# Modulation vectors of two transformer blocks: from TensorE products and partition sums to VectorE row sums

## The chip, the cores and the metric

One core of one Trainium2 chip. The metric is the device time of one execution in microseconds (us); the three runs of the kernel before gave 2533.99, 2531.1 and 2531.23, their median is 2531.23.

## What is computed

Two blocks, each of two layers, run one after the other on an input of 256 tokens by 1024 channels (f32). Every layer scales, shifts and gates its activations with vectors of 1024 that depend on a condition alone (6 chunks in a layer of the first block, 9 in one of the second):

```python
cond = silu(c)                                   # first block, [1, 1024]
mod = cond @ ada_w[layer] + ada_b[layer]         # [1, 6*1024]: shift, scale, gate (mixer), shift, scale, gate (FFN)
h = rmsnorm(x, norm_mix_g[layer]) * (1 + scale_m) + shift_m
x = x + gate_m * mixer(h)
h = rmsnorm(x, norm_ffn_g[layer]) * (1 + scale_f) + shift_f
x = x + gate_f * swiglu(h, ffn_w_in[layer], ffn_w_out[layer])
# second block: two streams (x with condition c_2, ctx with c_ctx_2), 9 chunks of 1024
m = (silu(cond) @ w_mod + b_mod).reshape(9, 1024)
```

The mixer is attention in layer 0 of the first block, a gated delta rule in layer 1, and a mix of Fourier, convolution and latent attention in the second block, which has an FFN before and one after it. `ada_w` is 2 x 1024 x 6144, `w_mod_2` 2 x 1024 x 9216; both are read from HBM once, as every other weight. The output is the x stream, 256 x 1024.

## The kernel before, in words

Activations lie transposed: eight tiles `x[k]` of 128 channels by 512 columns (256 of x, 256 of ctx). All weights are packed by the host into one array of units in the order in which they are used. `plan()` (L98) writes that order out by hand: a list of units, each a tile of 128 partitions by up to 1024 columns (512 KB). A "mat" unit is for matmuls; a "mod" or "acc" unit holds 128 rows of one chunk of a modulation matrix, so a chunk is eight units. `_evenly` (L57) strews the modulation units among the mat units of a stage, `_spread` (L47) puts one behind each.

`pump` (L373) runs up to 12 units ahead of the place in the plan. It issues the loads on SyncE's queue (L379) into two rings of buffers, 6 for mat units and 3 (`RAWM`) for modulation units, and it splits the next three mat units into a high and a low part, a cast on ScalarE (ACT, L391) and a subtraction on VectorE (DVE, L392); five such pairs of buffers exist. `get` (L397) hands a split unit to the matmuls, and before it `flush` (L405) works off the modulation units that stand ahead of it. A product of f32 quality is three matmuls on TensorE (PE), high x high, high x low and low x high (`mm3`, L414, lines 418 to 420). The tile framework sets the semaphores; each engine's queue runs in order.

A modulation unit is worked off in `mod_unit` (L482) in one of two ways. Kind "mod": four matmuls with 32 columns of the condition as weights, one for each quarter of 256 columns, summed in a PSUM buffer of their own over the eight units (`mod_rows`, L512, line 514). Kind "acc": an accumulator of 128x1024 takes on unit times condition, first by ACT (L501), then by a multiply-add on DVE (L508); in the first block's FFNs ACT multiplies (L505) and GpSimd (POOL) adds (L506). After the eighth unit `settle` (L517) sums over the partitions with four matmuls for each condition (L514 again). In both cases `mod_end` (L527) copies the result out (L531), transposes it with two matmuls (L534) so that the 1024 values lie as 128 partitions by 8 columns, and adds the bias (L542). Kind "mod" are chunks 1, 0, 4, 5 of layer 0 and 2, 3, 4, 5 of layer 1 of the first block; the other 22 chunks are "acc".

Stages in time, with the chunks that are worked off in them: start (1 and 0 of layer 0, before the first matmul unit), attention (2, 3 strewn, 4 and 5 behind the output projection), first FFN (layer 1's 0, 1), delta rule (2, 3, 4 strewn, 5 at its end), second FFN (second block's 1, 0), two-stream FFN (7 chunks), mix, two-stream FFN (5), two-stream FFN (6), mix, last FFN (none). The eight PSUM buffers are 3 "mm", 3 "ax", one "nm" for norms and one "md" for modulations.

At the start DVE computes the tables of the rotary embedding (`rope_tables`, L725, from L731 on) as soon as the positions have landed, then the norm (L568 to L570), the scaling of x (L897); the shift (L904 on ACT, L905 on DVE) needs chunk 0.

Of the kernel before, what the change touches and what calls it, by code (L numbers as in the profile page):

```python
# [34 lines left out]
def _mods(name, l, ch):  # L35
    return [("mod", (name, l, ch, kt), [(name, l, kt * 128, ch * 1024, 1024)]) for kt in range(KT)]
# [10 lines left out]
def _spread(units, mods, every):  # L47

    out, mods = mods[:3], mods[3:]
    for i, u in enumerate(units):  # L50
        out.append(u)
        if i % every == every - 1 and mods:
            out.append(mods.pop(0))
    return out + mods


def _evenly(units, mods, a, b, kind="acc"):  # L57

    n = len(units) - a - b
    out, k = [], 0  # L60
    for i, u in enumerate(units):
        out.append(u)
        while k < len(mods) and i >= a + k * n // len(mods):
            out.append((kind,) + mods[k][1:])
            k += 1
    return out
# [31 lines left out]
def plan():  # L98
# [15 lines left out]
    u += _evenly(q, A(0, 2, 3), 4, 0)  # L114
    q = []
# [4 lines left out]
    u += _spread(q, A(0, 4, 5), 1)  # L120
    u += _evenly(_ffn_units(("f", 0), "ffn_w_in", "ffn_w_out", 0), A(1, 0, 1), MODS_IN, MODS_OUT)
# [6 lines left out]
    u += _evenly(q, A(1, 2, 3, 4), 0, 4, "mod")  # L128
    u += A(1, 5)
# [16 lines left out]
def pack_weights(inp):  # L146
# [5 lines left out]
    arr["gdn_ab"] = ab  # L152
    arr["w_kr"] = np.tile(inp["w_in_2"][:, :, 1664:1696], (1, 1, 4))
# [25 lines left out]
def _col_plan():  # L179
    o = 0  # L180
    for name, n in (("norm_mix_g", 16), ("norm_ffn_g", 16), ("ada_b", 96), ("final_norm_g", 8),
                    ("gdn_conv", 96), ("gdn_norm_g", 1), ("a_log", 1), ("dt", 1), ("c", 8),
                    ("b_mod_2", 144), ("ffn1_norm_2", 16), ("mix_norm_2", 16), ("ffn2_norm_2", 16),
                    ("final_norm_2", 8), ("conv_w_2", 12), ("q_norm_2", 6), ("kv_norm_2", 4),
                    ("c_2", 8), ("c_ctx_2", 8), ("inv_freq", 1)):
        COLS[name] = (o, n)
        o += n
    return o
# [5 lines left out]
def pack_cols(i):  # L194
# [5 lines left out]
    def lay(v):  # L200
# [10 lines left out]
        "a_log": pad(i["gdn_a_log"][0]), "dt": pad(i["gdn_dt_bias"][0]), "c": _vec(i["c"][0]),  # L211
        "b_mod_2": lay(i["b_mod_2"]), "ffn1_norm_2": lay(i["ffn1_norm_2"]), "mix_norm_2": lay(i["mix_norm_2"]),
        "ffn2_norm_2": lay(i["ffn2_norm_2"]), "final_norm_2": _vec(i["final_norm_2"]), "conv_w_2": conv2,
        "q_norm_2": lay(i["q_norm_2"]), "kv_norm_2": lay(i["kv_norm_2"]), "c_2": _vec(i["c_2"][0]),
        "c_ctx_2": _vec(i["c_ctx_2"]), "inv_freq": invc,
# [72 lines left out]
class Unit:  # L288
    def __init__(self, hi, lo):
# [6 lines left out]
             "macc": (1024, 1), "sm": (512, 2), "e": (768, 1), "pt": (768, 1), "tab": (512, 1), "t": (256, 2)},  # L296
    "ffn1": {"hb": (KT * 520, 1), "t": (256, 3), "s": (256, 4), "hid": (512, 11), "macc": (1024, 2), "mprod": (1024, 1)},
# [12 lines left out]
class Builder:  # L310
    RAW, RAWM, SPL = 6, 3, 5
    LOOK, LOOKS = 12, 3

    def __init__(self, tc, es, a):
# [16 lines left out]
        self.unsettled = None  # L331
# [37 lines left out]
    def ax(self):  # L369
        return self.psum("ax", 3)  # L370
# [34 lines left out]
    def flush(self, n=len(PLAN)):  # L405

        end = self.pos + n
        while self.pos < min(end, len(PLAN)) and PLAN[self.pos][0] != "mat":
            self.pump()
            r = self.raw.pop(self.pos)  # L410
            self.mod_unit(PLAN[self.pos][1], r, PLAN[self.pos][0] == "acc")
# [70 lines left out]
    def mod_unit(self, key, r, acc):  # L482


        self.settle()
        name, l, ch, kt = key
        s0, ns = (0, 1) if name == "ada_w" else (1, 2)
        if kt == 0:
            if acc:
                self.macc = [self.t("macc") for _ in range(ns)]  # L490
            else:
                self.pmod = self.psum("md", 1)
        if not acc:
            self.mod_rows(self.pmod, self.cond[:, kt, :], r, kt == 0, kt == KT - 1)
            if kt == KT - 1:
                self.mod_end(key, self.pmod)
            return
        for s, a in enumerate(self.macc):
            w = self.cond[:, kt, s0 + s:s0 + s + 1]
            if kt == 0:  # L500
                self.nc.scalar.activation(a, r, AF.Copy, scale=w)  # L501
                continue
            if ns == 1 and "mprod" in self.tags:
                t = self.t("mprod")
                self.nc.scalar.activation(t, r, AF.Copy, scale=w)  # L505
                self.nc.gpsimd.tensor_tensor(a, a, t, op=OP.add)  # L506
            else:
                self.nc.vector.scalar_tensor_tensor(a, r, w, a, op0=OP.mult, op1=OP.add)  # L508
        if kt == KT - 1:
            self.unsettled = key, s0, self.macc  # L510

    def mod_rows(self, p, w, r, start, stop):  # L512
        for g in range(4):
            self.nc.tensor.matmul(p[32 * g:32 * g + 32, :256], w, r[:, 256 * g:256 * g + 256],  # L514
                                  start=start, stop=stop)

    def settle(self):  # L517

        if self.unsettled is not None:
            key, s0, acc = self.unsettled  # L520
            self.unsettled = None
            p = self.psum("md", 1)
            for s, a in enumerate(acc):
                self.mod_rows(p, self.pick[:, s0 + s, :], a, s == 0, s == len(acc) - 1)
            self.mod_end(key, p)

    def mod_end(self, key, p):  # L527
        nc = self.nc
        name, l, ch, _ = key
        e = self.sm.tile([128, 256], F32, name=f"me{name}{l}{ch}", tag="me", bufs=1)  # L530
        nc.scalar.copy(e, p[:, :256])  # L531
        q = self.psum("md", 1)
        for h in range(2):
            nc.tensor.transpose(q[:, 128 * h:128 * h + 128], e[:, 128 * h:128 * h + 128], self.ident)  # L534
        v = q[:, :256].rearrange("p (h g q) -> p g h q", h=2, g=4)
        ns = 1 if name == "ada_w" else 2
        t = self.keep(8 * ns, f"mod_{name}_{l}_{ch}")
        o, _ = COLS["ada_b" if ns == 1 else "b_mod_2"]
        nch = 6 if ns == 1 else 9
        b = self.cols[:, o + (l * nch + ch) * 8:o + (l * nch + ch) * 8 + 8]  # L540
        for s in range(ns):
            nc.vector.tensor_tensor(t[:, 8 * s:8 * s + 8].rearrange("p (g h) -> p g h", h=2),  # L542
                                    v[:, :, :, s if ns == 1 else 1 + s],
                                    b.rearrange("p (g h) -> p g h", h=2), op=OP.add)
            if ns == 2 and ch in (2, 8):
                nc.vector.tensor_scalar(t[:, 8 * s:8 * s + 8], t[:, 8 * s:8 * s + 8], 0.5, None, op0=OP.mult)
        self.mod[name, l, ch] = t
# [121 lines left out]
    def ffn(self, key, st, ns, A, B, gate, more, before_last=None):  # L669
# [55 lines left out]
    def rope_tables(self):  # L725
        nc = self.nc
        pi = self.sm.tile([128, T], I32, name="pos_i", tag="me", bufs=1)
# [211 lines left out]
    def gdn_gates(self, h):  # L939
        nc = self.nc  # L940
        p = self.gemm(self.get(("ab",)), h, 0, T)
        z, e, g = self.t("ga"), self.t("ga"), self.t("ga")
# [670 lines left out]
```

## Time and profile before

| | |
|---|---|
| median of three runs | 2531.23 us |
| the profiled execution, its own time | 2531.74 us |
| its span, first to last instruction | 2529.8 us |
| instructions | 39830 |
| moved by DMA | 407.59 MB, mean 161 GB/s |

Durations are those of the profiled execution. The profile's engines: PE is the matmul part of TensorE and PEld its weight loads, DVE is VectorE, ACT ScalarE, POOL GpSimd, SP SyncE, which only issues loads here. "L508" is line 508 of the kernel; a "<-" names what a tile is made from, or who ended a wait. A matmul in f32 shows as two records. Matmuls overlap, so the mean duration of one is longer than the time it takes of PE.

### The profile page before, as it was taken

How to read it: one execution, taken by the hardware profiler on the slowest of the kernel's cores; microseconds unless marked ns; L12 is line 12 of the kernel's file. 1: busy time of each engine (PE TensorE's matmuls, PEld its weight loads, DVE VectorE, ACT ScalarE, POOL GpSimd, SP SyncE). 2: the span in 40 equal slices, each digit the busy share in tenths (PEclk: the TensorE clock that was granted, in tenths of full speed). 3: DMA queues.
4: the chain of work that ended last, by engine and by line, in shares of the span. 5: the costliest groups of instructions: out<-in, count | busy, mean ns of one | idle time of the engine just before them, and what ended most of it. 6: DMA issues, size and time to landing. Idle time of an engine off the chain costs nothing.

```text
span 2529.8 us, 39830 instructions
## 1 busy us (share of the span) xinstructions
PE 2472.3 (98%) x15855; PEld 2155.0 (85%) x15855; DVE 1679.2 (66%) x2585; ACT 1127.6 (45%) x1957; POOL 199.8 (8%) x191
## 2 busy tenths in 40 slices
PE   7998999999999999999999999999999999999998
PEld 5878998988999877778886888888888888888998
DVE  6857768765887966775557564565556665576765
ACT  4556556665644532333437432323432323455544
POOL 1004100413100100000010100000100000111000
PEclk9999999999999999999999999999999999999999
DMA  9767656323876455554221243454244453232552
GB/s 339 269 206 250 205 188 226 109 92 122 302 244 207 169 166 174 193 189 151 90 71 42 76 153 108 144 173 147 101 158 156 154 173 125 84 127 84 199 184 93
DMA packets 117113, 407.59 MB, mean 161 GB/s; under 512 B 12992, under 2 KB 16320, under 8 KB 116928
## 3 DMA queue, kind: packets, MB, share of 16 engines
q1 hardware_dynamic: 113904, 402.30, 46.7%
q10 hardware_dynamic: 3024, 2.75, 0.4%
q8 instruction: 125, 2.05, 0.3%
q14 instruction: 60, 0.49, 0.1%
HBM read 403.95 MB, written 1.05 MB: 160 GB/s over the span
## 4 chain that ended last, share of the span: by engine, by line
PE 92%; DVE 3%; ACT 1%; DMA 1%; issue 1%; POOL 1%; DVEq 0%; ACTq 0%; POOLq 0%
PE pmm L418 26%; PE pmm L420 25%; PE pmm L419 25%; PE pmd L514 2%; PE pax L1070 2%; PE pmm L1392 1%; PE pax L420 1%; PE pax L419 1%; PE pax L418 1%; DMA r<-w 1%; PE pnm L1431 1%; PE pax L1402 1%; DVE l L392 1%; PE pnm L605 1%; PE pmm L427 0%
## 5 line engine op out<-in xcount | busy, mean ns | idle before, releaser
L391 ACT CAST h<-r 128x1024 fp32r<-128x1024 f32 (+2 forms) x543 | 548.7, 1016 | 1022.0 <-PE pmm L419 947.3
L392 DVE TENSOR_TENSOR l<-r,h 128x1024 fp32r<-128x1024 f32 (+2 forms) x543 | 656.4, 1214 | 307.8 <-ACT h L391 298.5
L418 PE MATMUL pmm<-h,h 128*128 128x512 f32 (+1 forms) x1916 | 669.8, 351 | 6.7 <-ACT h L638 2.3
L419 PE MATMUL pmm<-h,h 128*128 128x512 f32 (+1 forms) x1916 | 663.9, 347 | 2.0 <-DVE h L639 1.9
L420 PE MATMUL pmm<-h,l 128*128 128x512 f32 (+1 forms) x1916 | 664.5, 347 | 1.0 <-DVE l L392 1.0
L418 PEld LDWEIGHTS pmm<-h,h 128*128 128x128 f32 x1916 | 363.0, 190 | 63.6 <-issue 8.9
L419 PEld LDWEIGHTS pmm<-h,h 128*128 128x128 f32 x1916 | 363.0, 190 | 49.5 <-DVE h L639 3.2
L420 PEld LDWEIGHTS pmm<-h,l 128*128 128x128 f32 x1916 | 363.1, 190 | 47.5 <-DVE l L392 1.5
L418 PE MATMUL pmm<-hid,h 128*128 128x256 f32 (+1 forms) x1053 | 349.6, 332 | 0.0
L420 PE MATMUL pmm<-hid,l 128*128 128x256 f32 (+1 forms) x1053 | 347.5, 330 | 0.3 <-DVE l L392 0.3
L419 PE MATMUL pmm<-hid,h 128*128 128x256 f32 (+1 forms) x1053 | 347.5, 330 | 0.0
L508 DVE SCALAR_TENSOR_TENSOR macc<-r,cond,macc 128x1024 f32<-128x1024 f32 x266 | 329.8, 1280 | 0.1
L418 PE MATMUL pmm<-hb,h 128*128 128x258 f32 x1008 | 287.3, 285 | 7.6 <-DVE s L679 7.1
L420 PE MATMUL pmm<-hb,l 128*128 128x258 f32 x1008 | 285.8, 283 | 0.0
L419 PE MATMUL pmm<-hb,h 128*128 128x258 f32 x1008 | 285.3, 283 | 0.0
L418 PEld LDWEIGHTS pmm<-hid,h 128*128 128x128 f32 x1053 | 200.1, 190 | 20.2 <-ACT h L391 1.2
L420 PEld LDWEIGHTS pmm<-hid,l 128*128 128x128 f32 x1053 | 200.1, 190 | 18.6 <-DVE l L392 0.5
L419 PEld LDWEIGHTS pmm<-hid,h 128*128 128x128 f32 x1053 | 200.1, 190 | 18.3
L645 DVE SCALAR_TENSOR_TENSOR x<-pmm,mod_w_mod,x 128x256 f32<-128x256 f32 x188 | 84.5, 479 | 178.5 <-PE pmm L420 178.1
L418 PEld LDWEIGHTS pmm<-hb,h 128*128 128x128 f32 x1008 | 191.5, 190 | 10.4 <-DVE s L679 7.9
L420 PEld LDWEIGHTS pmm<-hb,l 128*128 128x128 f32 x1008 | 192.4, 191 | 0.4 <-issue 0.4
L419 PEld LDWEIGHTS pmm<-hb,h 128*128 128x128 f32 x1008 | 192.3, 191 | 0.3 <-DVE hb L628 0.2
(342 smaller groups left out, 2841.4 us busy)
## 6 DMA issues: line engine op xcount, KB each, us to landing
r<-w SPq DMA_DIRECT2D x665, 512.0 KB, 4.2
r<-w SPq DMA_DIRECT2D x96, 448.0 KB, 3.2
r<-w SPq DMA_DIRECT2D x16, 256.0 KB, 2.9
r<-w SPq DMA_DIRECT2D x6, 384.0 KB, 3.3
const<-const SPq DMA_DIRECT2D x2, 960.0 KB, 6.2
x<-xT ACTq DMA_DIRECT2D x8, 128.0 KB, 4.8
x<-ctxT ACTq DMA_DIRECT2D x8, 128.0 KB, 3.0
out<-x ACTq DMA_DIRECT2D x4, 128.0 KB, 2.1
```

Source lines behind the costliest of these rows:

```text
L391: nc.scalar.copy(h[:, :n], r[:, :n])
L392: nc.vector.tensor_tensor(lo[:, :n], r[:, :n], h[:, :n].bitcast(F32), op=OP.subtract)
L418: nc.tensor.matmul(out, wh, ah, start=start, stop=False)
L419: nc.tensor.matmul(out, wh, al, start=False, stop=False)
L420: nc.tensor.matmul(out, wl, ah, start=False, stop=stop)
L508: self.nc.vector.scalar_tensor_tensor(a, r, w, a, op0=OP.mult, op1=OP.add)
L514: self.nc.tensor.matmul(p[32 * g:32 * g + 32, :256], w, r[:, 256 * g:256 * g + 256], start=start, stop=stop)
L605: nc.tensor.matmul(p, self.ones, s[:, cg], start=tot == 1, stop=True)
L645: self.nc.vector.scalar_tensor_tensor(v, p[:, s * T - c0:s * T + T - c0], gate[:, 8 * s + m:8 * s + m + 1], v, op0=OP.mult, op1=OP.add)
L1070: nc.tensor.matmul(p[:, s], a[:, s], b[:, s], start=True, stop=True)
L1392: self.nc.tensor.matmul(s, q, k, start=True, stop=True)
L1402: self.nc.tensor.transpose(p[:, 128 * b:128 * b + 128], P[:, 128 * b:128 * b + 128], self.ident)
```

## The change

A modulation unit now holds 128 output channels by all 1024 inputs: the host packs the transposed matrices. The condition is loaded as a row and broadcast to all 128 partitions (128x1024), and passed through silu there. One DVE instruction multiplies the unit with the condition and writes out the sum of each row, which is one column of the modulation vector in the layout in which it is used; after eight units the bias is added. A unit of the second block is worked off twice, with the second and the third condition. The condition of the first block stays in SBUF; the two others are loaded again in each of the four FFNs that work off chunks of the second block. The accumulators, the partition sums, the copies and the transposes go.

The order of units: layer 0's chunks 2 to 5 are strewn evenly over attention and its output projection (32 units among 28), layer 1's 0, 1, 2 over the first FFN, 3, 4, 5 over the delta rule; the second block's stay where they were. The buffers for modulation units fall from 3 to 2, the PSUM buffer "md" becomes a fourth "ax", and some small tiles share tags with others.

```diff
 def _mods(name, l, ch):
-    return [("mod", (name, l, ch, kt), [(name, l, kt * 128, ch * 1024, 1024)]) for kt in range(KT)]
+    return [("mod", (name, l, ch, m), [(name + "_t", l, ch * 1024 + m * 128, 0, 1024)]) for m in range(KT)]
...
-    u += _evenly(q, A(0, 2, 3), 4, 0)
-    q = []
     for s in range(2):
         for m in range(0, 8, 2):
             q.append(("mat", ("ao", s, m), [("attn_w_out", 0, (4 * s + k) * 128, (m + i) * 128, 128)
...
-    u += _spread(q, A(0, 4, 5), 1)
-    u += _evenly(_ffn_units(("f", 0), "ffn_w_in", "ffn_w_out", 0), A(1, 0, 1), MODS_IN, MODS_OUT)
+    u += _evenly(q, A(0, 2, 3, 4, 5), 4, 0)
+    u += _evenly(_ffn_units(("f", 0), "ffn_w_in", "ffn_w_out", 0), A(1, 0, 1, 2), MODS_IN, MODS_OUT)
...
-    u += _evenly(q, A(1, 2, 3, 4), 0, 4, "mod")
-    u += A(1, 5)
+    u += _evenly(q, A(1, 3, 4, 5), 0, 4)
...
-    RAW, RAWM, SPL = 6, 3, 5
+    RAW, RAWM, SPL = 6, 2, 5
...
     def ax(self):
-        return self.psum("ax", 3)
+        return self.psum("ax", 4)
...
+    def condition(self, n, t):
+        src = self.a["cond"][n:n + 1, :]
+        self.nc.scalar.dma_start(t, bass.AP(tensor=src.tensor, offset=src.offset, ap=[[0, 128], [1, D]]))
+        self.act(t, t, AF.Silu)
+        return t
+    def conditions(self):
+        self.conds[1:] = [self.condition(n, self.t("cnd")) for n in (1, 2)]
+    def mod_unit(self, key, r):
+        nc = self.nc
+        name, l, ch, m = key
         ns = 1 if name == "ada_w" else 2
...
+        if m == 0:
+            self.mod[name, l, ch] = self.keep(8 * ns, f"mod_{name}_{l}_{ch}")
+        t = self.mod[name, l, ch]
         for s in range(ns):
...
+            o = self.t("junk") if s < ns - 1 else r
+            nc.vector.scalar_tensor_tensor(o, r, 1.0, self.conds[ns - 1 + s], op0=OP.mult, op1=OP.mult,
+                                           accum_out=t[:, 8 * s + m:8 * s + m + 1])
+        if m == KT - 1:
+            o, _ = COLS["ada_b" if ns == 1 else "b_mod_2"]
+            nch = 6 if ns == 1 else 9
+            b = self.cols[:, o + (l * nch + ch) * 8:o + (l * nch + ch) * 8 + 8]
+            for s in range(ns):
+                v = t[:, 8 * s:8 * s + 8]
+                nc.vector.tensor_tensor(v, v, b, op=OP.add)
+                if ns == 2 and ch in (2, 8):
+                    nc.vector.tensor_scalar(v, v, 0.5, None, op0=OP.mult)
...
             h = self.enter(st, ns, A, B, lead)
+        if conds:
+            self.conditions()
...
         nc.sync.dma_start(self.cols, a["cols"])
+        self.conds = [self.condition(0, self.keep(D, "cond")), None, None]
         self.phase("attn")
         self.rope = self.rope_tables()
```

Gone with it: `mod_rows`, `settle` and its calls, `mod_end`, the "acc" kind, `_spread`, the columns of the conditions in `cols`, and the condition and selection tiles with their POOL memsets and activations at the start (L1475 to L1483). The tags "macc" and "mprod" give way to "cnd" (two of 128x1024) and "junk" (one) in the FFN stages; `pos_i` moves to tag "u", the gates of the delta rule from "ga" to "vb".

## Rows read from the trace of the kernel before

**Rows 1.** The page: busy time of the engines, and the chain by engine.
```profile
PE 2472.3 (98%) x15855; PEld 2155.0 (85%) x15855; DVE 1679.2 (66%) x2585; ACT 1127.6 (45%) x1957; POOL 199.8 (8%) x191
...
PE 92%; DVE 3%; ACT 1%; DMA 1%; issue 1%; POOL 1%; DVEq 0%; ACTq 0%; POOLq 0%
```

**Rows 2.** Busy us (and instructions) by stretch: PE, PEld, DVE, ACT, POOL; clock, DMA.
```profile
0.00:32.40 32.40, 15.96 (x136) 5.77 (x136) 11.55 (x34) 8.76 (x20) 4.42 (x14) 1.00 0.96 358
32.40:178.00 145.60, 140.07 (x1040) 123.06 (x1040) 110.63 (x184) 79.19 (x141) 16.57 (x13) 0.98 0.69 250
178.00:388.00 210.00, 201.88 (x1659) 195.44 (x1658) 151.14 (x199) 116.61 (x201) 42.57 (x19) 0.98 0.64 222
388.00:640.00 252.00, 245.89 (x2015) 223.74 (x2014) 172.61 (x348) 156.20 (x316) 64.57 (x77) 1.00 0.42 138
640.00:848.00 208.00, 204.27 (x1689) 198.15 (x1690) 176.07 (x255) 117.00 (x214) 12.25 (x10) 0.99 0.68 237
848.00:1218.00 370.00, 370.00 (x1790) 302.00 (x1789) 252.76 (x305) 117.95 (x157) 6.48 (x5) 1.00 0.51 171
...
660.00:710.00 50.00, 50.00 (x420) 50.00 (x419) 49.88 (x67) 27.73 (x48) 0.00 (x0) 1.00 0.80 285
45.00:105.00 60.00, 57.08 (x413) 51.20 (x413) 56.85 (x106) 32.91 (x73) 10.12 (x7) 1.00 0.71 265
```

**Rows 3.** The same, of L514 alone (products, PE and PEld); last row L534 (transposes).
```profile
0.00:32.40 32.40, 13.09 (x128) 4.20 (x128) 1.00 0.96 358
32.40:178.00 145.60, 9.57 (x98) 2.60 (x98) 0.98 0.69 250
178.00:388.00 210.00, 5.65 (x63) 1.48 (x62) 0.98 0.64 222
388.00:640.00 252.00, 19.68 (x216) 5.65 (x216) 1.00 0.42 138
640.00:848.00 208.00, 5.34 (x72) 1.62 (x72) 0.99 0.68 237
...
sum 2529.80, PE 72.92 PEld 22.32; mean PE 6.63 PEld 2.03
...
sum 2529.80, PE 12.01 PEld 7.28; mean PE 1.09 PEld 0.66
```

**Rows 4.** The chain of waits in order of time: start us, us, what.
```profile
22.38 8.18 DMA r<-w
...
630.18 7.17 DMA r<-w
```

**Rows 5.** Groups by line: busy us, mean ns of one, idle us before.
```profile
L508 DVE SCALAR_TENSOR_TENSOR macc<-r,cond,macc 128x1024 f32<-128x1024 f32 x266 | 329.8, 1280 | 0.1
...
L817 DVE TENSOR_SCALAR s<-s 128x1 f32<-128x1 f32 (+1 forms) x56 | 8.4, 150 | 0.5
```

**Rows 6.** Busy us by stretch, of L508 alone (DVE).
```profile
32.40:178.00 145.60, 18.48 (x14) 0.98 0.69 250
...
640.00:848.00 208.00, 36.70 (x29) 0.99 0.68 237
848.00:1218.00 370.00, 119.44 (x97) 1.00 0.51 171
```

**Rows 7.** Timeline of DVE at the start: start us, us, what, [idle before].
```profile
5.83 0.29 DVE L731 CAST u<-pos_i 128x256 f32<-128x256 int32 x1 [4.92 <-DMA pos_i<-pos]
```

**Rows 8.** Timeline of DVE (first two) and POOL (last) in the first FFN.
```profile
205.50 1.21 DVE L392 TENSOR_TENSOR l<-r,h 128x1024 fp32r<-128x1024 f32 x1
...
210.98 3.40 DVE L392 TENSOR_TENSOR l<-r,h 128x1024 fp32r<-128x1024 f32 x1
...
210.88 2.41 POOL L506 TENSOR_TENSOR macc<-macc,mprod 128x1024 f32<-128x1024 f32 x1 [1.91 <-ACT mprod L505]
```

**Rows 9.** SyncE's queue: waits in all, times, longest us; the page: loads, us to landing.
```profile
SPq L379 <- DVE macc L508: 244.1, 121, 15.4
...
r<-w SPq DMA_DIRECT2D x665, 512.0 KB, 4.2
```

More of the change, by code (lines that the diff above doesn't have):

```diff
@@ L44, in _rows, with _evenly @@
     return ("mat", key, [(name, l, k * 128, m * 128, 128) for k in range(k0, k1)])
[L47 to L57, printed above, removed]
+def _evenly(units, mods, a, b):
     n = len(units) - a - b
@@ L63, in _evenly @@
         while k < len(mods) and i >= a + k * n // len(mods):
-            out.append((kind,) + mods[k][1:])
+            out.append(mods[k])
             k += 1
@@ L152, in pack_weights @@
     arr["gdn_ab"] = ab
+    for n in ("ada_w", "w_mod_2"):
+        arr[n + "_t"] = inp[n].transpose(0, 2, 1)
     arr["w_kr"] = np.tile(inp["w_in_2"][:, :, 1664:1696], (1, 1, 4))
@@ L181, in _col_plan @@
     for name, n in (("norm_mix_g", 16), ("norm_ffn_g", 16), ("ada_b", 96), ("final_norm_g", 8),
[L182 removed]
+                    ("gdn_conv", 96), ("gdn_norm_g", 1), ("a_log", 1), ("dt", 1),
                     ("b_mod_2", 144), ("ffn1_norm_2", 16), ("mix_norm_2", 16), ("ffn2_norm_2", 16),
                     ("final_norm_2", 8), ("conv_w_2", 12), ("q_norm_2", 6), ("kv_norm_2", 4),
[L185 removed]
+                    ("inv_freq", 1)):
         COLS[name] = (o, n)
@@ L410, in flush @@
             r = self.raw.pop(self.pos)
-            self.mod_unit(PLAN[self.pos][1], r, PLAN[self.pos][0] == "acc")
+            self.mod_unit(PLAN[self.pos][1], r)
             self.pos += 1
@@ L479, in act @@
         self.table_users.append(i)
[L482 to L525, printed above, removed]
@@ L527, in mod_end @@
-    def mod_end(self, key, p):
-        nc = self.nc
[L529 to L535, printed above, removed]
+    def condition(self, n, t):
[3 more added lines that the diff above has]
+        return t
@@ L541, in mod_end @@
         for s in range(ns):
[L542 to L547, printed above, removed]
+            o = self.t("junk") if s < ns - 1 else r
@@ L666, in project_out, with ffn @@
                     self.push(st, self.x[m], s * T, s * T + T)
-    def ffn(self, key, st, ns, A, B, gate, more, before_last=None):
+    def ffn(self, key, st, ns, A, B, gate, more, before_last=None, conds=True):
         nc = self.nc
@@ L726, in rope_tables @@
         nc = self.nc
-        pi = self.sm.tile([128, T], I32, name="pos_i", tag="me", bufs=1)
+        pi = self.t("u", dt=I32)
         nc.scalar.dma_start(pi, bass.AP(tensor=self.a["pos"].tensor, offset=self.a["pos"].offset,
@@ L941, in gdn_gates @@
         p = self.gemm(self.get(("ab",)), h, 0, T)
-        z, e, g = self.t("ga"), self.t("ga"), self.t("ga")
+        z, e, g = self.t("vb"), self.t("vb"), self.t("vb")
         dt, al = COLS["dt"][0], COLS["a_log"][0]
@@ L1474, in build @@
             nc.vector.memset(self.eps[e], e)
-        cond = self.cp.tile([128, KT, 32], F32, name="cond")
-        self.cond = cond
-        nc.gpsimd.memset(cond, 0.0)
-        self.pick = self.cp.tile([128, 3, 32], F32, name="pick")
-        nc.gpsimd.memset(self.pick, 0.0)
-        for i, n in enumerate(("c", "c_2", "c_ctx_2")):
-            nc.gpsimd.memset(self.pick[:, i, i:i + 1], 1.0)
-            o = COLS[n][0]
-            self.act(cond[:, :, i], self.cols[:, o:o + 8], AF.Silu)
         self.table(LOG_SET)
@@ L1525, in build @@
             st = self.ffn(("f", l), st, 1, A, B, gate, COLS["final_norm_g"][0] if l else None,
-                          before_last=context if l else None)
+                          before_last=context if l else None, conds=l == 1)
             self.dump(f"x{2 * l + 1}")
@@ L1569, in build @@
             A, B, gate = mods(w, l, 6, "ffn2_norm_2")
-            st = self.ffn(("f2", l), st, 1 if last else 2, A, B, gate, None)
+            st = self.ffn(("f2", l), st, 1 if last else 2, A, B, gate, None, conds=not last)
             self.dump(f"y{l}c")
@@ L1587, in arrays @@
     inp = {k: np.asarray(v) for k, v in inputs.items()}
-    r = {"w": pack_weights(inp), "cols": pack_cols(inp), "pos": np.ascontiguousarray(inp["positions"]).reshape(1, T)}
+    r = {"w": pack_weights(inp), "cols": pack_cols(inp), "pos": np.ascontiguousarray(inp["positions"]).reshape(1, T),
+         "cond": np.stack([inp["c"][0], inp["c_2"][0], inp["c_ctx_2"]])}
     for n, k in (("xT", "x"), ("ctxT", "ctx_2")):
```

17 lines of the change are left out of this document (4 added, 13 removed), and 4 rows, old and new, of the table PHASES.

## The prediction, made before any run of the changed kernel

> **What bounds the kernel now.** I read the page first, then busy time by stage, then the chain of waits. TensorE (PE) is busy 98% of the span and holds 92% of the chain that ended last; VectorE (DVE) is busy 66% [rows 1]. That says PE-bound, but it is an average. By stage [rows 2] DVE is far from even: it is 76% full in attention (32.4 to 178), 72% in the first FFN, 68% in the delta-rule stage, 85% in the second FFN and 68% in the two-stream FFN. Inside two stages it is full already: 56.85 of 60 us between 45 and 105, and 49.88 of 50 between 660 and 710, where PE still had work all the time (50.00) because its weight splits are made a few units ahead. So there are two resources near their limit, and the change moves work from the first to the second.
>
> What PE spends on modulations: the row products take 72.92 us and the transposes 12.01, of which 13.09 fall into the first 32.4 us [rows 3]. There PE was not the limit: the chain shows 8.18 us of waiting for weights from 22.38 on [rows 4]. A second such wait, 7.17 us, stands at 630.18, where eight modulation units follow each other with nothing between them [rows 4].
>
> **The price of the new operation.** 240 units become 96 row sums for the first block and 144 x 2 for the second, 384 in all, on DVE; 266 multiply-adds of the same shape (two f32 inputs of 128x1024) go [rows 5]. One of those lasts 1280 ns, and 97 of them took 119.44 us between 848 and 1218, so one costs 1.23 us of DVE [rows 5, 6]. A row sum that is written out on DVE is not in the trace. Low bound: 1.23 us. High bound: twice the duration, and 0.15 us for reading the sum out, the duration of a 128x1 operation on DVE: 2 x 1.28 + 0.15 = 2.71 us [rows 5]. I take 1.23 + 0.15 = **1.38 us**, because the row with the same inputs, the same output and one more operand is nearest.
>
> The rule that speaks against this: the Trainium skill, page "Vector Engine (DVE) Microarchitecture Reference", section "Points that are easy to get wrong", says that this instruction with two non-bf16 sources in SBUF runs at half throughput, since no read port is left for the accumulator. The row at 1280 ns has two such sources and no halving, but it writes out no accumulator, so the trace doesn't decide; by the rule the kernel becomes slower (third rival).
>
> **The sum, stage by stage**, against the profiled execution: its span 2529.8, its own time 2531.74, 0.5 us above the median 2531.23 of the three runs. Where DVE is the fuller engine I take its work divided by 0.95, the fill of the row 45 to 105 [rows 2].
>
> 1. *Start, to 32.4 us.* Sixteen units go from PE to DVE, and DVE has the rope tables there too. DVE starts at 5.83 [rows 7], when the positions have landed, and has 11.55 us of its own [rows 2]; with 16 x 1.38 = 22.1 it is done at 39.5. Before, the shift could start at 32.4. **+7.** Covered only if row sums are put into the 5.8 us before the rope tables, which need a condition that has just been loaded. The condition's load goes on ACT's queue ahead of the positions and of x; I cost that at nothing while the weights are the later arrival [rows 4].
> 2. *Attention, 32.4 to 178.* PE loses 9.57 us of products [rows 3]. DVE loses 18.48 us (14 multiply-adds [rows 6]) and gets 32 x 1.38 = 44.2, because the last two chunks, products on PE before, are now spread here: 110.63 - 18.48 + 44.2 = 136.3, over 0.95 is 143.5, against 145.6. **-2**: PE's gain is not collected.
> 3. *First FFN, 178 to 388.* PE idled 210 - 201.88 = 8.1 us and did 5.65 us of products [rows 2, 3]. One cause of the idling shows in a pair of rows: a POOL sum of 2.41 us starts at 210.88, and a DVE split, begun 0.1 us later, takes 3.40 where the one at 205.50 took 1.21 [rows 8]. Fourteen such POOL sums go, each up to 2.2 us of DVE, say 20 in all; 24 x 1.38 = 33.1 come: 151.14 - 20 + 33 = 164, under PE's 196. **-13.**
> 4. *Delta-rule stage, 388 to 640.* PE loses 19.68 + 1.6 us (four of 30 transposed chunks, 4 x 12.01 / 30) [rows 3]. DVE goes from 172.61 to 172.61 + 33.1 = 205.7, over 0.95 is 216, under PE's 230.7. PE's bound would give -21. Here DVE's short steps release PE's next product, and one row sum ahead of them in the in-order queue delays them by up to 1.38 us; I take two thirds, **-14**, which includes the wait at 630.18.
> 5. *Second FFN, 640 to 848.* PE loses 5.34 + 1. DVE: 176.07 - 36.70 + 32 x 1.38 = 183.5, over 0.95 is 193 against PE's 201.5 [rows 2, 3, 6]; but 50 us of it are at 100% now, and they get more. **-4.**
> 6. *All later stages.* PE loses what is left of the products, 72.92 - 13.09 - 9.57 - 5.65 - 19.68 - 5.34 = 19.6, and of the transposes 16 chunks, 6.4. DVE in the fullest, 848 to 1218: 252.76 - 119.44 + 112 x 1.38 = 288 of 360, so PE stays the bound. Against it stand the conditions, loaded and passed through ACT again in four stages; ACT is busy 118 of 370 us there, so I charge 1 us each. **-22.**
>
> Edits that cost nothing: POOL's memsets at the start go (POOL is 8% busy [rows 1]); a fourth PSUM buffer in place of the products' own can only help; the table storage and gate tiles that change their tag are not used at the same time as their new neighbours.
>
> Sum: 7 - 2 - 13 - 14 - 4 - 22 = -48; 2531.74 - 48 = 2483.7, which against the median is **2483 us**.
>
> **What the added wait holds up.** A row sum waits on DVE for its load, and behind it in DVE's queue stand the weight splits and the PSUM reads that PE needs. The buffers for these loads fall from 3 to 2. SyncE's queue already waited 244.1 us, 121 times, for the multiply-adds to release theirs, and a load takes 4.2 us to land [rows 9]. With two buffers a pair of units needs at least 4.2 + 1.38 = 5.6 us, 2.8 each; attention has 145.6 / 32 = 4.5 us for each on average, but its projections ask for more than one per weight unit. On the other side DVE never waited before a multiply-add (0.1 us in all [rows 5]). I cost it at nothing, with the rival below as the other end.
>
> **Rivals.**
> - *PE stays the bound everywhere* (DVE's queue is elastic enough, as from 660 to 710). Then the start costs nothing and the stages give 9.6 + 13.8 + 21.3 + 8 + 6 + 26, some 85 to 90 us: **2443**. For it: PE had no idle time in the fullest stretch. Against it: the arithmetic of the start and of attention.
> - *DVE waits for the loads* in the stages with one stream. There are 32 + 24 + 24 + 16 = 96 units; at 0.5 us each the gain is gone, **2531**, and at 1 us, a quarter of a landing, it is 2580. For it: SyncE's 121 waits; against it: the 0.1 us above.
> - *The row sum runs at half rate* (the other side). Place: DVE, in every stage. At 2.71 us: start +28, attention +43, first FFN -3, delta rule -2, second FFN +30, 848 to 1218 +90, the rest about -8: some **2710**. It decides from about 1.95 us on: there start and attention cost 16 + 17, the second FFN 4, 848 to 1218 nothing, and 13 + 14 + 14 come back elsewhere, a draw.
>
> **Chances.** Forecast (2455 to 2511) 0.60; PE-bound everywhere 0.12; loads or DVE's order eat the gain 0.16; half rate 0.12. The measurement tells 0.2%, about 5 us, from no change. Faster: the first two and a little of the third, 0.73; no change 0.06; slower 0.21: the half rate, and more than half of the loads' case. The range, 2440 to 2560, takes in the second case, most of the third and a price of the row sum up to about 2.1 us; the half rate and the worst of the third stay outside.
>
> **What would show it.** Right: no products or transposes of modulations on PE; 384 row sums at 1.2 to 1.3 us, with a short read behind each; DVE busy some 1679 - 330 - 20 + 384 x 1.38 = 1860 us; the first projection some 7 us later than at 32.4; attention's end near 183; the first FFN's idle time gone; no load wait at the delta rule's end; the two-stream FFNs each 6 to 10 us shorter. Wrong: row sums above 1.9 us, idle DVE time put down to loads before them, SyncE waiting far longer on their release, or splits that come late for PE in the two-stream stages.

## The result, and the profile after

The changed kernel takes **2504.36 us** (median of four runs, 2502.62 to 2509.48) against 2531.93 of the kernel before on the same chip: a ratio of **0.9893** (95% interval 0.9876 to 0.9910). That is 27.6 us faster, where 48 were forecast; 2483 was 21 us too low, and the range of 2440 to 2560 holds the result. The profiled execution is the slowest of the four (span 2507.6, own time 2509.48), so its stages below add up to 22 us, not 27.6. One of the four executions of e10 below took 6089.86 us against 2479.83 to 2483.56 for the others, and its time is given without it.

The page of the changed kernel, the lines that answer to [rows 1]:

```profile
PE 2401.4 (96%) x14963; PEld 2137.6 (85%) x14963; DVE 1779.4 (71%) x3087; ACT 1071.7 (43%) x1879; POOL 166.0 (7%) x172
...
PE 71%; DVE 15%; DMA 9%; issue 3%; ACT 2%; POOL 1%; SPq 0%; DVEq 0%; ACTq 0%; POOLq 0%
```

PE lost 70.9 us of busy time, but the span fell by only 22.2. (The 72.92 + 12.01 us of products and transposes that are gone were counted alone, with ends that overlap other matmuls; without them PE's busy time in the kernel before is 2406.4 of 2472.3, so 65.9 us were theirs only.) PE's idle time grew from 57.5 to 106.2 us. The chain says who has it: DVE went from 3% to 15%, DMA from 1% to 9%.

Where did it arise? I cut both executions at the same places: the first weight product of attention, and then the first of the two products that close each stage's sum of squares. The differences in the length of each stage, after minus before, against the forecast:

| us | start | attention | first FFN | delta rule | second FFN | first two-stream FFN | all behind it |
|---|---|---|---|---|---|---|---|
| before | 34.0 | 144.1 | 208.2 | 253.8 | 205.2 | 370.7 | 1302.9 |
| after | 44.8 | 141.9 | 202.8 | 247.9 | 197.3 | 370.6 | 1291.4 |
| difference | +10.9 | -2.2 | -5.5 | -5.9 | -7.9 | -0.1 | -11.5 |
| forecast | +7 | -2 | -13 | -14 | -4 | -22 for these two | |

Busy time in the same stretches of the changed kernel (columns as in [rows 2]):

```profile
0.00:44.80 44.80, 2.08 (x4) 1.18 (x4) 33.01 (x70) 13.60 (x22) 5.09 (x9) 1.00 0.88 320
44.80:186.70 141.90, 133.18 (x940) 121.64 (x941) 129.87 (x237) 73.22 (x135) 14.05 (x13) 0.98 0.75 267
186.70:389.50 202.80, 195.74 (x1587) 193.45 (x1585) 175.84 (x294) 97.05 (x177) 6.53 (x5) 0.98 0.85 290
389.50:637.40 247.90, 231.00 (x1799) 221.68 (x1799) 174.32 (x344) 156.98 (x317) 66.85 (x77) 0.98 0.29 95
637.40:834.70 197.30, 193.00 (x1592) 191.52 (x1592) 173.95 (x284) 108.95 (x203) 14.03 (x10) 1.00 0.68 222
834.70:1205.30 370.60, 363.58 (x1685) 303.24 (x1686) 270.62 (x439) 105.81 (x142) 6.48 (x5) 0.98 0.56 178
```

The groups of the new instruction (busy us, mean ns of one | idle before), which answer to [rows 5]:

```profile
L492 DVE SCALAR_TENSOR_TENSOR junk<-r,cnd 128x1024 f32<-128x1024 f32 x144 | 176.2, 1224 | 28.6 <-DMA r<-w 24.7 <-ACT cnd L465 3.0
...
L492 DVE SCALAR_TENSOR_TENSOR r<-r,cond 128x1024 f32<-128x1024 f32 x96 | 116.9, 1221 | 32.0 <-DMA r<-w 31.5
...
L492 DVE DVE_READ_ACCUMULATOR r<-r,cond 128x1 f32 x96 | 7.7, 80 | 0.0
```

So the price is not where the gain went. A row sum lasts 1.22 us, its read another 80 ns, nearly all of which lies under the row sum's end; all 384 take 469 us of DVE, 1.22 us each. That is below the 1.38 taken and at the low bound. The rule that spoke against the change (the Trainium skill, page "Vector Engine (DVE) Microarchitecture Reference", section "Points that are easy to get wrong": half throughput for this instruction with two non-bf16 sources in SBUF) does not hold here: 1024 f32 columns from two such sources with the accumulator take 1221 ns, where the multiply-add of the same shape without it took 1280 [rows 5].

What the groups also show is idle time before the row sums: 56 us of DVE waiting for loads, where before it was 0.1. And the same stretches for the row sums alone show that they don't run where the plan puts them (two instructions for each):

```profile
44.80:186.70 141.90, 42.93 (x70) 0.98 0.75 267
186.70:389.50 202.80, 55.27 (x90) 0.98 0.85 290
389.50:637.40 247.90, 0.00 (x0) 0.98 0.29 95
637.40:834.70 197.30, 39.55 (x64) 1.00 0.68 222
```

The plan gives 32, 24, 24 and 32 row sums to these stages; 35, 45, 0 and 32 ran. The order in which instructions are issued is settled by the scheduler when the program is built; my reading, which e1 tests, is that a load that has a free buffer of its own kind is put ahead of weight loads that wait for theirs. The whole set of the delta rule is loaded and summed during the first FFN.

### The profile page after: what moved, and what is told of

The parts are those of the page before. It is cut to its first block, busy times and chain, and to the rows that moved or that the text cites. A ratio compares the mean times of both kernels' runs of the same rounds, so it can differ in the third digit from the quotient of the medians.

```text
span 2507.6 us, 38408 instructions
## 1 busy us (share of the span) xinstructions
PE 2401.4 (96%) x14963; PEld 2137.6 (85%) x14963; DVE 1779.4 (71%) x3087; ACT 1071.7 (43%) x1879; POOL 166.0 (7%) x172
## 4 chain that ended last, share of the span: by engine, by line
PE 71%; DVE 15%; DMA 9%; issue 3%; ACT 2%; POOL 1%; SPq 0%; DVEq 0%; ACTq 0%; POOLq 0%
PE pmm L407 19%; PE pmm L406 19%; PE pmm L408 19%; DMA r<-w 8%; DVE l L380 4%; DVE r L492 3%; DVE junk L492 2%; PE pax L1027 2%; PE pmm L1349 1%; PE pax L408 1%; PE pax L407 1%; PE pax L406 1%; PE pnm L1388 1%; PE pax L1359 1%; ACT h L379 1%
## 5 line engine op out<-in xcount | busy, mean ns | idle before, releaser
L380 DVE TENSOR_TENSOR l<-r,h 128x1024 fp32r<-128x1024 f32 (+2 forms) x543 | 644.0, 1190 | 231.8 <-ACT h L379 224.5
L492 DVE SCALAR_TENSOR_TENSOR junk<-r,cnd 128x1024 f32<-128x1024 f32 x144 | 176.2, 1224 | 28.6 <-DMA r<-w 24.7
```

The lines of the kernel that those rows point to most:

```text
L380: nc.vector.tensor_tensor(lo[:, :n], r[:, :n], h[:, :n].bitcast(F32), op=OP.subtract)
L492: nc.vector.scalar_tensor_tensor(o, r, 1.0, self.conds[ns - 1 + s], op0=OP.mult, op1=OP.mult, accum_out=t[:, 8 * s + m:8 * s + m + 1])
```

## The experiments

My theory (A) was that this early, bunched order loses the gain: row sums, and their waits for loads, stand in DVE's in-order queue ahead of splits and PSUM reads. Rivals: the row sums' own DVE time costs it wherever they run (B); two buffers make loads late (C). Later a fourth was added: what was removed from PE was not all on the path (D). All differences below are to the stages of the kernel before, cut as above:

| us | start | attention | first FFN | delta rule | second FFN | first two-stream FFN | all behind it |
|---|---|---|---|---|---|---|---|
| changed kernel | +10.9 | -2.2 | -5.5 | -5.9 | -7.9 | -0.1 | -11.5 |
| e1 loads in plan order | +10.6 | +0.2 | -16.7 | +1.6 | -2.6 | -12.1 | -17.4 |
| e2 rope tables first | +12.2 | -1.8 | -5.4 | -6.0 | -7.8 | -2.8 | -17.3 |
| e3 short sums | +1.5 | -6.3 | -16.8 | -5.2 | -3.0 | -12.1 | -18.3 |
| e4 no sums | +1.1 | -6.7 | -17.5 | +20.2 | -6.6 | -12.1 | -18.3 |
| e5 = e1, start's order | +5.4 | +3.9 | -14.4 | +3.7 | -4.3 | -13.8 | -16.0 |
| e6 before, fewer products | +1.6 | 0.0 | -0.4 | -3.0 | -2.5 | -1.0 | +0.1 |
| e7 = e1, three buffers | +10.8 | -5.1 | -15.2 | +2.9 | -3.8 | -13.8 | -18.2 |
| e8 = e1, units moved | +10.7 | +0.5 | -13.4 | -5.8 | -1.1 | -11.7 | -17.0 |
| e9 changed, filler on PE | +10.6 | -1.7 | -5.9 | +6.1 | -7.1 | -6.0 | -14.2 |
| e10 = e7 and e8 | +10.7 | -3.7 | -15.4 | -6.5 | -4.8 | -13.7 | -18.2 |
| e11 = e10, start's order | +6.2 | +4.9 | -15.8 | -5.6 | -5.5 | -12.2 | -18.2 |
| e12 = e11, tables on POOL | +20.3 | -0.8 | -15.7 | -8.2 | -6.1 | -12.2 | -18.3 |

**e1, loads in plan order.** A dependency without a semaphore, from each weight load to the one before it, fixes SyncE's order:

```diff
-            nc.sync.dma_start(t[:, :n], ...)
+            d = nc.sync.dma_start(t[:, :n], ...)
+            if self.last is not None:
+                self.after(d, self.last)
+            self.last = d
```

> Every weight load is put behind the load that precedes it in the plan, on SyncE's queue; nothing else changes. Theory A (the gain is lost because modulation loads, and so row sums, run ahead of the plan and fill DVE in bursts): the 24 row sums of the delta-rule stage return to it, the 112 of the first two-stream FFN spread over its whole length, its PE stall near 1055 us goes (about 9 us) and most of the 7.6 us that PE idles in the first FFN; 2485 to 2493 us. Rival B (the 384 row sums cost what they cost, wherever they run): 2500 to 2508 us. Rival C (loads that come late are the cost): slower, 2510 or more, since a load can no longer be put ahead.

Measured: **2495.47 us**, ratio 0.9851 (0.9835 to 0.9868), 9 us under the changed kernel, between theory A's range and rival B's. Busy time by stage in e1, from the first FFN on:

```profile
188.80:380.40 191.60, 190.89 (x1588) 190.38 (x1586) 155.77 (x251) 95.86 (x175) 5.93 (x5) 1.00 0.73 254
380.40:635.80 255.40, 232.87 (x1794) 222.64 (x1794) 198.73 (x389) 156.71 (x316) 68.48 (x77) 0.97 0.39 132
635.80:838.40 202.60, 195.08 (x1596) 193.66 (x1596) 174.50 (x285) 109.23 (x204) 13.03 (x10) 0.99 0.64 221
838.40:1197.00 358.60, 358.60 (x1686) 300.24 (x1687) 272.33 (x439) 106.25 (x142) 6.47 (x5) 1.00 0.52 182
```

and the row sums alone in the first two of these stretches:

```profile
188.80:380.40 191.60, 33.90 (x55) 1.00 0.73 254
380.40:635.80 255.40, 29.51 (x42) 0.97 0.39 132
```

Theory A holds in the FFNs: 27 sums instead of 45 in the first FFN, PE full (190.89 of 191.60), 11 us more gained; in the first two-stream FFN PE is busy all the time with the same 112 sums, 12 us more gained. There the changed kernel had this stall (PE, PEld, DVE, ACT, POOL, granted clock, DMA):

```profile
1015.00:1048.00 33.00, 33.00 (x146) 27.09 (x145) 32.08 (x55) 8.58 (x12) 0.00 (x0) 1.00 0.70 228
1048.00:1058.00 10.00, 4.89 (x22) 3.67 (x20) 7.99 (x12) 1.30 (x2) 0.00 (x0) 0.89 0.75 222
1058.00:1068.00 10.00, 8.33 (x23) 6.29 (x24) 9.36 (x17) 1.56 (x2) 0.00 (x0) 0.60 0.66 210
```

and these waits from 838 to 1207, PE's for a split of the hidden values, and ACT's, just ahead of it, for a PSUM read on DVE:

```profile
ACT hid L444 <- DVE s L644: 59.3, 13, 9.3
...
PE pmm L406 <- ACT hid L444: 6.6, 1, 6.6
```

A full queue is not all of it: the last row sum ahead of that read, at 1056.98, had waited for its load. The chain in the stall (start us, us):

```profile
1051.56 5.39 DMA r<-w
```

But half of that was given back: the delta rule, with 21 of its sums in it again, is 7.5 us longer, attention 2.4, the second FFN 5.3. For the last, the chain of e1 (start us, us) has a load wait as that FFN begins:

```profile
642.16 9.57 DMA r<-w
```

The running ahead hurt the FFNs and helped the delta rule. Theory A was one part of it. A stage of a single profile can move by 6 us without an edit in it (e2's last column), so what is read of the stages is what repeats: the delta rule takes 245.6 to 248.2 us in the six kernels where its full sums run elsewhere (the changed one, e2, e8, e10, e11, e12) and 255.4 to 257.5 in the three where they run in it (e1, e5, e7).

**e2, rope tables first.** `self.after(row_sum, last_operation_of_the_tables)` for every row sum.

> The row sums are put behind the last operation of the rope tables on DVE. Theory A (at the start the rope tables stand behind row sums, so the Sin, the table load and the norm come late): first matmul at 37 to 39 us in place of 44.8, the whole 2496 to 2499 us. Rival (16 row sums and their loads set the start by themselves): first matmul at 43 to 45 us, 2502 to 2507 us.

Measured: 2501.04 us, ratio 0.9873 (0.9858 to 0.9887), not told apart from the changed kernel. The first matmul came at 46.1, later, not at 37 to 39: theory A missed here. DVE's timeline of e2, with the first operation of the tables, the first row sum and the bias behind the last:

```profile
7.59 0.29 DVE L689 CAST u<-u 128x256 f32<-128x256 int32 x1 [6.69 <-DMA u<-pos]
...
16.12 1.21 DVE L492 SCALAR_TENSOR_TENSOR r<-r,cond 128x1024 f32<-128x1024 f32 x1
...
45.38 0.16 DVE L501 TENSOR_TENSOR mod_ada_w<-mod_ada_w,cols 128x8 f32<-128x8 f32 x1
```

The tables only changed places with the sums. From the first sum to the bias DVE worked for 29 us with 0.6 us of idle time.

**e3, short sums, and e4, no sums.**

```diff
-            ...(o, r, 1.0, self.conds[ns - 1 + s], ...
+            ...(o[:, :64], r[:, :64], 1.0, self.conds[ns - 1 + s][:, :64], ...
```

and, in e4, `nc.vector.memset(t, 0.0)` at the first unit of a chunk in place of the row sums.

> Each row sum reads only the first 64 of its 1024 columns, so the modulations are not those of the reference; the loads, the waits and the order stay. DVE is then busy some 400 us less. If the cost is DVE's time in the queue (A and B): 2445 to 2460 us. If it is the waits for loads at the head of DVE's queue (C): 2490 to 2505 us.

> The row sums are left out and the modulations are zero before the bias; the loads stay. The floor that any order of the row sums can reach. If PE is the bound once DVE is relieved: 2435 to 2450 us, so the row sums cost 55 to 70 us in the changed kernel. If the products on PE were largely hidden in other waits before: 2465 to 2490 us. The difference to the short sums is the price of the waits for loads.

Measured: e3 **2475.78 us**, ratio 0.9774 (0.9758 to 0.9790); e4 2491.56, ratio 0.9836 (0.9821 to 0.9850). The short sum's group in e3:

```profile
L492 DVE SCALAR_TENSOR_TENSOR r<-r,cnd 128x64 f32<-128x64 f32 x144 | 32.1, 224 | 6.9 <-ACT cnd L465 2.6
```

e3 takes some 350 us of work off DVE (its busy time is 1430.0) and leaves the loads; each buffer comes free about 1 us sooner. That is worth 29 us, most of what the row sums' DVE time costs, and lies between the two expected ranges. It also settles the other end. With row sums nearly free the kernel gains 57 us; by the profiles the span is 60 us shorter and PE's busy time 83 (2389.1). So some 23 us of PE's work had not been on the path, or something else took its place there (D): PE's idle time grows by 15 us in the start, where the prediction had not counted on PE's products, and by 11 in the delta rule. e1's first three FFNs equal e3's within 0.4 us, so there, in plan order, the row sums cost nothing; what they cost lies in the start (9 us), attention (6) and the delta rule (7). e4 lies above both of its ranges. Without a reader the loads' buffers come free at once, and all loads of modulations run ahead of the weights; in the delta rule, DMA is then 85% busy, load waits hold 55.7% of the chain, and PE is at 0.93 of its clock:

```profile
363.30:637.30 274.00, 238.74 (x1795) 228.66 (x1795) 173.54 (x343) 155.24 (x315) 67.01 (x77) 0.93 0.85 285
```

So e4 is no floor, and its difference to e3 is not the price of waits: it is a third thing, loads in a bad order.

**e5, the start's order.** On e1: `rope_tables()` is called behind the shift, and no weight is split while the sixteen row sums are being issued (`while FIRST <= self.pos and ...`).

> The kernel with loads in plan order, and at the start two things moved on DVE: the rope tables are made behind the shift, and no weight is split before the sixteen row sums. Theory (DVE's queue is full from 20 us on, and 8 us of rope tables and 4.7 us of splits stand ahead of the last row sum): first matmul at 36 to 39 us in place of 44.6, 2487 to 2491 us in place of 2495.5. Rival (the loads set the start): the first matmul stays at 43 to 45 us and the time at 2494 to 2497.

Measured: 2497.00 us, ratio 0.9860 (0.9845 to 0.9874). The first matmul came at 39.3, near what the theory said, and yet the time is the rival's: attention, with the tables and splits in it now, is 3.7 us longer, the delta rule 2.1, the first FFN 2.3.

**e6, the kernel before with fewer products in the delta rule.** The test of D by itself; DVE gets nothing in return.

```diff
+        if not acc and l == 1:
+            self.nc.tensor.matmul(self.pmod[:32, :16], self.cond[:, kt, :], r[:, :16], ...)
+            ...
+            return
         if not acc:
```

> The kernel before, with the products of the delta-rule stage's 32 units cut to one of 16 columns each, and their transposes and bias left out, so that these modulations are zero; the loads stay. PE loses some 20 of its 246 us in the stage, and DVE gets nothing in return. Theory (the products lay in time in which PE would have waited for the other engines, and kept its clock up): the stage becomes 3 to 8 us shorter, granted clock below 1.00 somewhere in it, 2525 to 2530 us. Rival (PE was the bound there, and it is the row sums and their order that lose the gain): 18 to 22 us shorter, 2511 to 2515 us.

Measured: 2526.08 us, ratio 0.9974 (0.9965 to 0.9984). The stage in the kernel before, first the instructions of the modulations' PSUM tile alone (PE, PEld, DVE, ACT):

```profile
386.30:640.10 253.80, 22.02 (x231) 6.72 (x230) 0.64 (x4) 1.48 (x4) 1.00 0.42 139
```

then all of it:

```profile
386.30:640.10 253.80, 247.59 (x2025) 224.49 (x2024) 173.94 (x349) 157.48 (x320) 64.57 (x77) 1.00 0.42 139
```

The same tile in e6:

```profile
387.50:638.30 250.80, 6.30 (x67) 3.70 (x66) 0.17 (x1) 0.37 (x1) 0.97 0.43 141
```

and two pieces of the stage, then all of it:

```profile
387.00:400.00 13.00, 10.13 (x59) 8.39 (x59) 10.19 (x24) 6.63 (x14) 0.00 (x0) 0.74 0.67 217
448.00:460.00 12.00, 8.83 (x42) 6.86 (x41) 9.59 (x26) 7.12 (x18) 1.46 (x2) 0.72 0.78 264
...
387.50:638.30 250.80, 239.58 (x1862) 226.96 (x1861) 171.29 (x344) 154.89 (x314) 65.09 (x77) 0.97 0.43 141
```

22.02 - 6.30 = 15.7 us of products are gone when they are counted alone (20 were expected). Their ends overlap other matmuls: PE's busy time without them is 230.4 us before and 235.1 in e6, so 247.59 - 230.4 = 17.1 us were theirs only before and 239.58 - 235.1 = 4.5 in e6, and 12.6 are gone. The stage is **3.0 us** shorter. PE's busy time fell by only 8.0, so the other matmuls take 4.6 us longer by the second count and 7.7 by the first; the granted clock, 1.00 all through the stage before, is 0.97, with two pieces near 0.73 where PE was idle for a fifth to a quarter of the time (a mix of its levels of 2.4 and 1.2 GHz). PE's idle time grew by 5.0. 3.0 + 4.6 + 5.0 = 12.6, or 3.0 + 7.7 + 5.0 = 15.7. The products had filled gaps and had kept the clock up. The whole kernel gains 6.1 us by the medians; 2.5 us of the profile's gain stand in the second FFN, where nothing was edited.

The changed kernel shows the same idle time: 17.1 to 22.0 us of products gone, 5.9 gained, 16.9 us idle in place of 6.2, and 0.5 to 5.4 us more for the other matmuls, at a granted clock of 0.98. Two pieces of its stage:

```profile
388.00:400.00 12.00, 7.83 (x39) 6.83 (x38) 9.99 (x21) 5.59 (x13) 0.00 (x0) 0.73 0.44 139
...
448.00:460.00 12.00, 8.47 (x46) 7.07 (x44) 11.24 (x32) 8.34 (x22) 1.46 (x2) 0.86 0.00 1
```

**e7, three buffers on e1.** `RAW, RAWM, SPL = 5, 3, 5` in place of 6, 2, 5.

> The kernel with loads in plan order, and one of the six weight buffers given to the modulations (5 and 3 in place of 6 and 2). Rival C (two buffers are why row sums come late in attention, the delta rule and the second FFN): those three give back 10 to 15 us, 2480 to 2486 us. Theory A (order and DVE's fill, not the buffers): within 4 us of 2495.5.

Measured: 2491.41 us, ratio 0.9836 (0.9821 to 0.9851): 4.1 us under e1, between the two ranges, and the intervals of the two overlap. Attention gets 5.3 us back, the second FFN 1.2, the delta rule nothing (-1.3). So two buffers were part of the cost in attention (e10 against e8 repeats it, 4.2 us); elsewhere nothing stands out from the few us by which stages move. One weight buffer less came with it, so this is not the third buffer alone.

**e8, the delta rule's units in the first FFN.** On e1, `A(1, 0, 1, 2, 3, 4, 5)` is spread over the first FFN, none over the delta rule.

> The kernel with loads in plan order, and the 24 modulation units of the delta-rule stage planned into the first FFN, which then has 48, evenly spread. Theory (the first FFN has room on DVE when they come evenly, the delta-rule stage has none because its short DVE steps release PE): the delta rule 6 to 8 us shorter, the first FFN at most 3 longer, 2488 to 2493 us. Rival (48 are too many, however they are spread): the first FFN 8 to 12 us longer as in the changed kernel, 2496 to 2501 us.

Measured: 2494.55 us, ratio 0.9858 (0.9836 to 0.9881): the whole is not told apart from e1, but the stages are: the delta rule 7.4 us shorter, the first FFN 3.3 longer. 48 units planned into that FFN, 46 of which ran there, cost 3 us; the 45 that ran there in the changed kernel cost 11. It is their order, not their number.

**e9, filler.** Four products of 128x256, which nobody reads, ahead of each of the delta rule's 49 units.

> The kernel with loads in plan order, and on PE four products of 128x256 that nobody reads ahead of each of the delta-rule stage's 49 units, 196 in all, some 21 us of PE; one PSUM buffer moves to them. Theory (PE has idle time in that stage, and more work on it keeps the granted clock up): the stage 0 to 6 us longer than 255.4, 2495 to 2502 us. Rival (PE is the bound there): 17 to 21 us longer, 2512 to 2517 us.

The kernel that ran was the changed kernel with the filler, without the plan order of loads, so it is to be held against 2504.36 and against a delta rule of 247.9. Measured: 2510.81 us, ratio 0.9911 (0.9895 to 0.9928). The stage:

```profile
389.40:649.20 259.80, 252.41 (x1989) 242.88 (x1989) 174.86 (x344) 156.42 (x312) 63.71 (x77) 0.99 0.28 92
```

21.4 us more on PE (252.4 - 231.0) make it 12 us longer (the whole kernel, by the medians, 6.5); the rest goes into PE's idle time, which falls from 16.9 to 7.4. Neither 0 to 6 nor 17 to 21: the gaps take less than half of work that stands at fixed places, the rest delays what follows.

**e10 to e12, what helps together.** e10 is e1 with e7's and e8's edits; e11 adds e5's; e12 makes the tables on POOL (`nc.gpsimd`, the multiply-adds as two instructions) early, in place of on DVE behind the shift.

> Loads in plan order, three buffers for modulations and five for weights, and the delta rule's 24 units planned into the first FFN. If the gains of the two single steps add up (5 us in attention, 1 to 3 from the move): 2487 to 2491 us. If the first FFN with 48 units takes the third buffer's gain back: 2491 to 2496 us.

> The same with the start's order of e5 (rope tables behind the shift, no split before the sixteen row sums). If attention gave the 5 us of the start back only because its loads had two buffers: first matmul at 39 us, 2482 to 2486 us. If DVE has no room for the tables and splits that now come in attention: the same as e10 within 2 us.

> The kernel of e11, but with the rope tables made on GpSimd (POOL) at the start in place of on DVE behind the shift, so some 7 us of DVE work are gone from the start and from attention alike. Theory (from 9 us to the end of attention DVE is the bound, so work moved within that stretch gains nothing and work taken out of it does): attention ends at 180 to 184 us in place of 185.0 (e10) and 189.2 (e11), 2473 to 2479 us. Rival (POOL's operations slow DVE's down as its sums did in the first FFN of the kernel before, or hold up the norm): attention ends at 185 to 190 us, 2479 to 2486 us.

Measured: e10 **2480.00 us**, ratio **0.9799** (0.9783 to 0.9816), better than expected and faster than both kernels (15.5 us under e1, where e7 and e8 alone give 4.1 and 0.9; why they give more together is not shown); e11 2479.95, ratio 0.9800 (0.9785 to 0.9814), the same; e12 2492.67, ratio 0.9844 (0.9826 to 0.9861). Start and attention of e10, then of e11:

```profile
0.00:44.60 44.60, 2.07 (x4) 1.17 (x4) 32.95 (x70) 13.58 (x22) 4.71 (x9) 1.00 0.91 333
44.60:185.00 140.40, 132.37 (x940) 121.20 (x940) 127.86 (x235) 72.99 (x136) 16.77 (x13) 0.99 0.71 262
```

```profile
0.00:40.20 40.20, 2.09 (x5) 1.20 (x5) 25.91 (x56) 10.95 (x18) 5.10 (x9) 1.00 0.88 314
40.20:189.20 149.00, 135.20 (x938) 122.87 (x938) 135.55 (x252) 78.30 (x142) 19.57 (x13) 0.96 0.71 263
```

7 us of DVE work moved from the first stretch to the second, where DVE is over 90% full: the time moves along. That attention ends 4 us later is not to be leaned on, as the profiled execution of e11 is 5.7 us above its median. e12 was to take it out of both, and failed at another place: POOL needs until 39 us for the tables, ACT does their Sin first and the norm behind them, and seven of the sixteen row sums, beside POOL's operations, take 1.35 to 1.78 us in place of 1.23. ACT's timeline of e12:

```profile
39.63 0.42 ACT L469 ACTIVATE tab<-u 128x256 f32<-128x256 f32 x1 [6.12 <-POOL u L711]
...
41.36 0.47 ACT L469 ACTIVATE y<-pnm,eps1e-06_162 128x256 f32<-128x256 f32 x1
```

The norm at 41.4, the first matmul at 54.2. Attention ended at 197.5, beyond even the rival's figure, though both things that the rival names did happen. Whether DVE is the only bound from the start to attention's end is therefore not shown.

## Why the prediction was right in sign, and where its steps failed

- **The price** (1.38 us, bounds 1.23 to 2.71): 1.22 measured, just under the low bound. Taking the nearest row served well; the 0.15 added for the read was too much, since the read lies under the sum's end.
- **Start** (+7): +10.9. The mechanism, DVE full of row sums and tables, was right; the sum was too small by a later beginning and by splits that come ahead of the last sum and its bias. With short sums (e3) the start is only 1.5 us longer, so some 9 us are the row sums' DVE time. DVE's and ACT's timelines of the changed kernel:

```profile
9.14 1.23 DVE L492 SCALAR_TENSOR_TENSOR r<-r,cond 128x1024 f32<-128x1024 f32 x1 [8.23 <-DMA r<-w]
10.29 0.08 DVE L492 DVE_READ_ACCUMULATOR r<-r,cond 128x1 f32 x1
10.29 0.29 DVE L688 CAST u<-u 128x256 f32<-128x256 int32 x1
...
39.51 1.21 DVE L380 TENSOR_TENSOR l<-r,h 128x1024 fp32r<-128x1024 f32 x1
40.65 1.21 DVE L492 SCALAR_TENSOR_TENSOR r<-r,cond 128x1024 f32<-128x1024 f32 x1
```

```profile
29.21 0.42 ACT L465 ACTIVATE tab<-u 128x256 f32<-128x256 f32 x1 [7.08 <-DVE u L704]
29.65 1.28 ACT L452 ACT_TABLE_LOAD   x1
30.94 0.47 ACT L465 ACTIVATE y<-pnm,eps1e-06_155 128x256 f32<-128x256 f32 x1
```

  The tables' first operation, at 5.83 before [rows 7], comes at 10.29, behind a row sum that DVE has waited for until 9.14; the last of the sixteen sums begins at 40.65, behind a split, and two more splits come ahead of the bias. The step "I cost that at nothing" failed as well: with the condition's load ahead of them the positions are there at 7.59 (e2), 1.8 us later, and the norm's logarithm, at 19.66 before, has to wait for the tables' Sin until 30.94.
- **Attention** (-2): -2.2, by luck: two errors cancel. DVE's work came out at 129.87 us, not 136.3, and its fill at 0.92, not 0.95; e7 gains 5 us here with a third buffer, so the fill was partly a matter of buffers.
- **First FFN** (-13): -5.5, and -16.7 in e1. The term was right for the work as planned; the step that failed is "24 x 1.38 = 33.1 come". 45 came, because their loads ran ahead of the plan.
- **Delta rule** (-14): -5.9 with none of its sums in it, and +1.6 in e1 with 21 of them in it. This is the step that was wrong in kind. "I take two thirds" of PE's 21 us supposed that the products stood on the path because PE was busy 98% and DVE only 68% [rows 2]; e6 shows that taking out most of them is worth 3.0 us in the stage, and 6.1 in all, when DVE gets nothing at all. The 21 us were also too many, as the products' rows count ends that overlap other matmuls: 17.1 us were theirs only. The load wait at the stage's end, which was to go with them, stayed too (chain of waits of the changed kernel, against [rows 4]):

```profile
622.05 2.74 DMA r<-w
627.09 6.79 DMA r<-w
```

- **Second FFN** (-4): -7.9, and -2.6 in e1; the 5.3 between them go with loads that were done ahead.
- **Later stages** (-22): -11.6, and -29.5 in e1. "PE stays the bound" is true of the stretch on average, 270.62 of 370.60 us for DVE; in the first two-stream FFN it is 12 us longer than in e1 all the same. 7.0 of these are PE's idle time, nearly all in one stall behind a full DVE and a late load; the other 5.0 are matmuls that took longer, at a granted clock of 0.98 in place of 1.00.
- **The rivals.** "PE stays the bound everywhere" is excluded by e3, which is at 2476, not at 2443, with sums that cost next to nothing. "DVE waits for the loads" was right in what it named (56 us of waits, and SyncE waiting 363.7 us on the row sums, 157 times, against the 244.1 of [rows 9]), but its price of 0.5 us for each of 96 units was too high: with the order mended, a third buffer gives back some 4 us in all (e7). "I cost it at nothing" was too low by as much, and by the load in the stall above. The half rate did not happen. SyncE's waits in the changed kernel:

```profile
SPq L367 <- DVE r L492: 363.7, 157, 20.0
```

What stays open: what besides DVE's fill sets the end of attention, which hardly moves when the first matmul comes 5 us sooner (e5 against e1); why e10 gains more than its parts; and how much of the delta rule's loss a filler at the right places could regain.

## What to carry to other kernels

A busy share of 98% does not say that work taken from an engine shortens the stage: in a stage of short steps that hand over between engines, PE's removed products can leave gaps and a lower clock, as here, so try the removal by itself first. And count what leaves an engine by the time that was its alone, not by durations that overlap. When work moves to an engine with an in-order queue, its time matters less than where it stands in that queue; read in the trace where the scheduler really put it, stage by stage, and if loads have a buffer kind of their own, tie their order to the plan. Then plan the moved work into stages with room (here the FFNs, where 48 to 112 planned row sums cost 3 us or nothing) and out of those where the receiving engine releases the next step.

## What of the hardware was not expected

- The row sum with accumulator, two f32 sources of 128x1024, takes 1221 to 1224 ns, less than the multiply-add's 1280 [rows 5]; at 128x64 it takes 224 to 236.
- The read of the accumulator, 80 ns, costs next to nothing: it begins before the row sum's end (10.29 against 9.14 + 1.23 in the changed kernel), and the next instruction begins with it.
- Taking 12.6 to 15.7 us of matmuls out of a stage of 253.8 us made the others there 4.6 to 7.7 us longer, at a granted clock of 0.97 in place of 1.00.
